# Tile 1 of a sparse expert layer moves from a fully dense to a half-gathered, half-dense form

## The chip, the cores and the metric

The kernel runs on one core of a Trainium2 chip. The metric is the device time of one execution in microseconds. Five engines work beside each other: TensorE (PE: matmuls, with PEld its weight loads), VectorE (DVE), ScalarE (ACT), GpSimd (POOL) and SyncE (SP, which here only issues DMAs). Each engine runs its own instructions strictly in the order in which the built program holds them.

## The reference, cut to what matters

One encoder layer over 1024 tokens of 1024 features: an attention and pooling block, then the PEER layer that the change is about. Each token picks 128 of 16384 experts (8 heads, 16 each), each with a gate.

```
q = (ht @ wq).reshape(T, PEER_HEADS, 2, PEER_HALF)
sc = jnp.einsum('thpd,hpnd->thpn', q, subkeys, preferred_element_type=jnp.float32)
...
u = jnp.take(u_tab, eb, axis=0)
vv = jnp.take(v_tab, eb, axis=0)
act = jax.nn.gelu(jnp.einsum('tkd,td->tk', u, xb), approximate=False)
return jnp.einsum('tk,tkd->td', gb * act, vv)
```

The first product is u times token, the second is the sum of the v rows weighted by gate times activation.

## The kernel before

The tokens are eight tiles of 128. Each tile's PEER layer is done in one of two ways.

- **Gathered** (tiles 0, 6, 7): for each of the 128 picks, GpSimd issues an indirect DMA that brings one u row (4 KB) for each of the 128 tokens into a row buffer (512 KB a gather, line 165), and VectorE multiplies it with the token's vector and sums (line 186). Then 128 gathers of v rows, which VectorE adds into the output with a weight (line 193). That is 256 gathers a tile. The row buffers form a ring, and a gather into a buffer waits until VectorE has done with the buffer's last row. The ring has two buffers in the first part (GB0), three (GBUFS: two named row, one rowx) once `wide` is set, and six in the last part. The gathers of all tiles stand in one list, in order, and `flow(x)` takes the next of them at a given rate between other work.
- **Dense** (tiles 1 to 5): all 16384 experts are computed, in 128 blocks of 128. `u_mm(b)` multiplies a block of u with the five tiles' 640 tokens, as two halves of 320 columns, each 24 matmuls (three terms of a split fp32 product, eight chunks of the features). The Gelu of it is multiplied with the gates, which `gates(i)` has written as a dense table (expert, token) to DRAM as `gd`, and `v_chunk` multiplies the results of four blocks with v: for each of the five tiles and each half of the features 12 matmuls of 512 columns (line 966). ACT splits u into a rounded part, and GpSimd makes the rest (line 240).

The program runs through these stages: **front** (first product `first`, attention and output projection `second` for groups of tiles; tile 0's routing `zero` beside the tiles 1 and 2), **scores** (the routing products of the other seven tiles, with `top16` on VectorE), **gates** (for each tile in ORDER: `topk`, and for a dense tile `gates`), **back** (the dense blocks with `u_mm`, `v_chunk`). 68 of the 128 u blocks are computed ahead of the back (`ahead()`), beside scores and gates, and kept in DRAM as `ad`. A list scheduler with a timeline of its own fixes each engine's order when the program is built, so the order of one engine can be read, and differs from the order of the source.

The lines that the steps rest on:

```
issue(n + GBUFS - 1 + (XBUFS if st.get("more") else 0))
r = rows.pop(n)
vec = st["vec"]
if s == 0:
    V.scalar_tensor_tensor(r, r, 1.0, vec, op0=OP.mult, op1=OP.mult, accum_out=st["act"][:, k:k + 1])
```

Of the kernel before, what the change touches and what calls it, by code (L numbers as in the profile page):

```python
# [31 lines left out]
GSCALE = 32768.0  # L32
EARLY = 0.2
EARLY2 = 0.4
EARLY3 = 0.45
ORDER = (6, 1, 2, 3, 4, 5, 7)
PER = 8
# [3 lines left out]
YS = 26  # L41
# [7 lines left out]
ULP = 4  # L49
FIRST = ((0, 1, 2), (3, 4), (5, 6), (7,))  # L50
ZN = 80
# [4 lines left out]
SPLIT0 = 1  # L56
AT = (-1, 0, 2, 3)
GB0 = 2
# [9 lines left out]
XT = 1  # L68
LOS = (1, 1, 2, 2)
LOS2 = (1, 1, 1, 2, 1)  # L70
# [14 lines left out]
GATHERED = (0, 6, 7)  # L85
DENSE = (1, 2, 3, 4, 5)
ND = len(DENSE)
DT = ND * P
NH = DT // 2
GBUFS = 3  # L90
# [33 lines left out]
def body(tc, ctx, a):  # L124
# [20 lines left out]

    gathers = [(i, s, k) for i in GATHERED for s in range(2) for k in range(128)]
    tabs = (a["u"], a["v"])
# [22 lines left out]
    def gather_step():  # L170
# [14 lines left out]
        if s == 0:  # L185
            V.scalar_tensor_tensor(r, r, 1.0, vec, op0=OP.mult, op1=OP.mult, accum_out=st["act"][:, k:k + 1])  # L186
            if k == P - 1:
                gl = st["G"].tile([P, P], F32, name="act", bufs=2)
                S.activation(gl, st["act"], AF.Gelu)
                V.tensor_tensor(gl, gl, EX[i][1], op=OP.mult)  # L190
                st["gl"] = gl
# [25 lines left out]
    after = dict(zip([None] + soon + later, soon + later + [None]))  # L217
    ad = DR.tile([KEYS, P, DT], F32, name="ad")

# [33 lines left out]
    def open_u():  # L253
        B = U["u"] = ctx.enter_context(tc.tile_pool(name="dense", bufs=1, side="right", reuse_waits="tile"))
        hh = U["hh"] = B.tile([P, DC, DT], F32R, name="hh")
        hl = U["hl"] = B.tile([P, DC, DT], F32R, name="hl")
        for j, i in enumerate(DENSE):
            halves(i, hh[:, :, j * P:(j + 1) * P], hl[:, :, j * P:(j + 1) * P])
        return hh, hl

    def u_mm(b):
        uh, ul = (t.rearrange("p (c e) -> p c e", c=DC) for t in us.pop((b, None)))
        pa = []
        after["turn"] = not after.get("turn")
        for n in range(2):
            p = PS.tile([P, 512], F32, name="pu", bufs=2) if b in soon or after["turn"] else ps()
            for k, (l, r) in enumerate(((uh, U["hh"]), (uh, U["hl"]), (ul, U["hh"]))):
                for d in range(DC):
                    E.matmul(p[:, :NH], l[:, d, :], r[:, d, n * NH:(n + 1) * NH],  # L269
                             start=(k == 0 and d == 0), stop=(k == 2 and d == DC - 1))  # L270
            pa.append(p)
        return pa

    def ahead():
        if AHEAD:
            with tc.high_priority(offset=-AHP):
                load(after[None])
                split(after[None])
        for b in soon:
            with tc.high_priority(offset=-AHP):  # L280
                if after[b] is not None:
                    load(after[b])
                pa = u_mm(b)
                if after[b] is not None:
                    split(after[b])
                t = U["u"].tile([P, DT], F32, name="wr", bufs=WRB)
                for n in range(2):
                    S.activation(t[:, n * NH:(n + 1) * NH], pa[n][:, :NH], AF.Gelu)  # L288
                nc.scalar.dma_start(ad[b], t)
            yield  # L290
# [10 lines left out]
def front(tc, ctx, a, env):  # L301
# [84 lines left out]
    def late_consts():  # L386
# [218 lines left out]
    def second(tiles):  # L605
# [22 lines left out]
        for m, i in enumerate(tiles):  # L628
# [28 lines left out]
    def topk(i):  # L657
# [29 lines left out]
        for s in range(2):  # L687
# [13 lines left out]
            yield  # L701
        keep = i in GATHERED
        gate = (C if keep else X).tile([P, PH, 16], F32, name=f"gate{i}" if keep else "gate", bufs=1)
# [11 lines left out]
        if keep:  # L715
            EX[i] = (idx, gate.rearrange("p h r -> p (h r)"))
        else:
            p = ps()
# [11 lines left out]
    def scores(tiles, cols, split):  # L730
# [45 lines left out]
        for i in tiles:  # L776
            carry["top", i] = vv[i], ix[i]

    def gates(i):
        j = DENSE.index(i)  # L780
        ekT, gT = carry["G", i]
        for q in range(P // TCH):
            sg = M.tile([P, KEYS, TCH], F32, name="stage", bufs=2)
            for r in range(TCH // 8):
                t0 = q * TCH + r * 8

                pairs = lambda x: x.rearrange("p (q w) -> p q w", w=2)[:, :, None, :].to_broadcast([P, 4, P, 2])
                ob = []
                for s in range(2):
                    o = M.tile([P, 4, P, 2], F16, name=f"ob{s}", bufs=OB)  # L790
                    V.tensor_tensor(o, pairs(ekT[:, s, t0:t0 + 8]), late["iote"][:, None, :, :].to_broadcast([P, 4, P, 2]),  # L791
                                    op=OP.is_equal)
                    ob.append(o)
                yield
                og = []
                for s in range(2):
                    o = M.tile([P, 4, P, 2], F16, name=f"og{s}", bufs=OB)
                    V.tensor_tensor(o, ob[1], pairs(gT[:, s, t0:t0 + 8]), op=OP.mult)  # L798
                    og.append(o)
                yield  # L800
                for h in range(2):
                    p = ps()
                    for t in range(4):
                        for s in range(2):
                            E.matmul(p[:, t * KEYS:(t + 1) * KEYS], ob[0][:, h * 2 + t // 2, :, t % 2], og[s][:, h * 2 + t // 2, :, t % 2],
                                     start=(s == 0), stop=(s == 1))
                    S.activation(sg[:, :, r * 8 + h * 4:r * 8 + h * 4 + 4], p.rearrange("p (t e) -> p e t", t=4),
                                 AF.Copy, scale=1.0 / GSCALE)
                yield
# [55 lines left out]
    X.open("late")  # L865
    rest = GATHERED[1:]
# [4 lines left out]
    cols = [(hh[:, :, :NH], hl[:, :, :NH]), (hh[:, :, NH:], hl[:, :, NH:]), (gh, gl)]  # L871
    merge([(scores(DENSE + rest, cols, True), 2 * PH * (NT - 1 + 3)), (ahead, AHEAD1)], EARLY2)
# [15 lines left out]
def back(tc, ctx, a, env):  # L888
# [34 lines left out]
    def u_block(b):  # L923
        if b not in soon and after[b] is not None:
            load(after[b])
        if b % CHUNK == 0 and b // CHUNK + 1 < NCH:
            gload(b // CHUNK + 1)
        wr = B.tile([P, DT], F32, name="wb", bufs=WB)
        if b in soon:
            nc.sync.dma_start(wr, ad[b])  # L930
            pa = [wr]
        else:
            pa = [p[:, :NH] for p in u_mm(b)]
            pace(2)
            if after[b] is not None:
                split(after[b])
            for n in range(2):
                S.activation(pa[n], pa[n], AF.Gelu)
            pace(1)
        g = gts[b // CHUNK]  # L940
        wh = B.tile([P, DT], F32R, name="wh", bufs=CHUNK + WX)
        wl = B.tile([P, DT], F32R, name="wl", bufs=CHUNK + WX)
        w, hn = DT // len(pa), NTC // len(pa)
        for n, p in enumerate(pa):
            V.tensor_tensor(wr[:, n * w:(n + 1) * w].rearrange("p (n t) -> p n t", t=TCH),  # L945
                            p.rearrange("p (n t) -> p n t", t=TCH),
                            g[:, n * hn:(n + 1) * hn, b % CHUNK, :], op=OP.mult)
        m = b % CHUNK
# [3 lines left out]
        S.activation(wh, wr, AF.Copy)  # L952
        pace(3 if b not in soon else 0.5)
        V.tensor_tensor(wl, wr, wh, op=OP.subtract)  # L954
# [84 lines left out]
```

## Time and profile before

| | us |
|---|---|
| median of 3 runs | 2683.09 (2680.38 to 2690.16) |
| the profiled execution's own time | 2683.19 |
| its span, first to last instruction | 2681.3 |
| busy in the span: PE, DVE, POOL, ACT | 2483.0, 2295.3, 1412.3, 925.3 |

The span is what the stages below are cut from; 1.9 us lie around it. A busy share of an engine is an average over stages: what ends last in a stage is read from that stage. Matmuls are pipelined, so the time of one is longer than the step from one to the next.

### The profile page before, as it was taken

What the parts mean: (1) busy time and instruction counts of PE and PEld (TensorE: products, weight loads), DVE (VectorE), ACT (ScalarE), POOL (GpSimd) and SP (SyncE); (2) the same over time, 40 slices, a digit from 0 to 9 for tenths busy, and PEclk for the clock granted to TensorE, in tenths of its full rate; (3) what the DMA queues carried; (4) which work ended last, traced back from release to release, by engine and by line L of the source; (5) the groups of instructions that cost most, each with busy time, mean ns of one, the idle gap of its engine ahead of it and who ended that gap; (6) DMA issues with size and microseconds to landing.
All of it is one profiled execution on the core that took longest, in us unless ns stands there. A gap on an engine that the chain in (4) does not pass through costs nothing.

```text
span 2681.3 us, 41366 instructions
## 1 busy us (share of the span) xinstructions
PE 2483.0 (93%) x14627; PEld 2198.3 (82%) x14627; DVE 2295.3 (86%) x4668; ACT 925.3 (35%) x1699; POOL 1412.3 (53%) x1380
## 2 busy tenths in 40 slices
PE   7889886999989789888959999999999999999999
PEld 6657654999988789887858888888888888888887
DVE  4657776679989899997959999899998998989998
ACT  5744553432223344444423222222223222222221
POOL 1101566665556665656645565465564655645653
PEclk9889988999999899999979999999999999999999
DMA  7645578987778776878799999899998999989987
GB/s 246 208 146 182 190 255 261 336 297 233 242 230 262 239 224 209 261 243 260 240 356 342 358 348 328 322 339 333 346 350 316 359 357 331 346 313 359 345 315 264
DMA packets 321504, 770.23 MB, mean 287 GB/s; under 512 B 26736, under 2 KB 123920, under 8 KB 317200
## 3 DMA queue, kind: packets, MB, share of 16 engines
q0 software_dynamic: 110592, 402.70, 42.3%
q1 hardware_dynamic: 114352, 287.55, 31.0%
q10 hardware_dynamic: 96352, 77.34, 8.9%
q8 instruction: 114, 1.87, 0.3%
q14 instruction: 94, 0.77, 0.1%
HBM read 687.53 MB, written 79.95 MB: 286 GB/s over the span
## 4 chain that ended last, share of the span: by engine, by line
PE 60%; DVE 18%; DMA 10%; issue 3%; POOL 2%; ACT 1%; ACTq 1%; SPq 0%; DVEq 0%; POOLq 0%
PE pt L966 15%; PE ps L966 15%; PE pu L269 14%; PE pt L269 3%; PE ps L269 3%; DMA row<-u,idx 3%; DVE vec L193 3%; DVE og L798 3%; DVE ob L791 2%; PE pt L360 2%; DVE row L186 2%; DMA row<-v,idx 1%; DMA wb<-ad 1%; DMA rowx<-v,idx 1%; DMA ad<-wr 1%
## 5 line engine op out<-in xcount | busy, mean ns | idle before, releaser
L240 POOL TENSOR_TENSOR ul<-ur,uh 128x256 fp32r<-128x256 f32 x512 | 456.7, 923 | 155.4 <-ACT uh L235 74.0
L165 POOL DMA_INDIRECT row<-v,idx x301 | 329.2, 1094 | 337.7 <-DVE vec L193 218.3
L165 POOL DMA_INDIRECT row<-u,idx x306 | 315.1, 1030 | 295.7 <-DVE row L186 169.2
L193 DVE SCALAR_TENSOR_TENSOR vec<-row,act,vec 128x1024 f32<-128x1024 f32 x301 | 384.9, 1279 | 36.0 <-DMA row<-v,idx 33.8
L186 DVE SCALAR_TENSOR_TENSOR row<-row,vec 128x1024 f32<-128x1024 f32 x306 | 368.0, 1211 | 37.6 <-DMA row<-u,idx 37.6
L269 PE MATMUL pu<-hh,uh 128*128 128x320 f32 x1568 | 282.7, 319 | 39.9 <-ACT wr L288 39.8
L269 PEld LDWEIGHTS pu<-hh,uh 128*128 128x128 f32 x1568 | 246.7, 193 | 53.4 <-ACT wr L288 47.5
L269 PE MATMUL pu<-hh,ul 128*128 128x320 f32 x1568 | 278.7, 314 | 5.8 <-POOL ul L240 5.8
L269 PE MATMUL pu<-hl,uh 128*128 128x320 f32 x1568 | 283.0, 317 | 0.0
L269 PEld LDWEIGHTS pu<-hh,ul 128*128 128x128 f32 x1568 | 243.9, 191 | 11.9 <-POOL ul L240 7.4
L269 PEld LDWEIGHTS pu<-hl,uh 128*128 128x128 f32 x1568 | 248.2, 193 | 2.6
L235 ACT ACTIVATE uh<-ur 128x1024 fp32r<-128x1024 f32 x128 | 135.5, 1059 | 266.6 <-PE pu L269 193.6
L966 PE MATMUL pt<-v0h,wh 128*128 128x512 f32 x384 | 151.9, 396 | 30.8 <-ACT wh L952 26.1
L952 ACT ACTIVATE wh<-wb 128x640 fp32r<-128x640 f32 x128 | 92.0, 733 | 246.0 <-DVE wb L945 126.3
L235 ACT ACTIVATE v0h<-vr 128x512 fp32r<-128x512 f32 x128 | 80.5, 631 | 246.9 <-DMA vr<-v 135.1
L966 PE MATMUL pt<-v0h,wl 128*128 128x512 f32 x384 | 151.8, 395 | 3.2 <-DVE wl L954 3.0
L966 PE MATMUL pt<-v0l,wh 128*128 128x512 f32 x384 | 150.4, 392 | 0.0
L966 PE MATMUL ps<-v1h,wh 128*128 128x512 f32 x384 | 149.5, 389 | 0.0
L966 PE MATMUL ps<-v1h,wl 128*128 128x512 f32 x384 | 149.5, 389 | 0.0
L966 PE MATMUL ps<-v1l,wh 128*128 128x512 f32 x384 | 149.5, 389 | 0.0
L165 POOL DMA_INDIRECT rowx<-v,idx x83 | 89.6, 1080 | 98.6 <-DVE vec L193 45.9
L969 DVE TENSOR_TENSOR acc<-pt,acc 128x512 f32<-128x512 f32 x160 | 109.3, 683 | 36.7 <-PE pt L966 36.4
(265 smaller groups left out, 5867.5 us busy)
## 6 DMA issues: line engine op xcount, KB each, us to landing
ur<-uT SPq DMA_DIRECT2D x128, 512.0 KB, 5.0
vr<-v SPq DMA_DIRECT2D x256, 256.0 KB, 5.9
gd<-stage ACTq DMA_DIRECT2D x20, 2048.0 KB, 12.3
g<-gd SPq DMA_DIRECT2D x32, 1280.0 KB, 9.2
ad<-wr ACTq DMA_DIRECT2D x68, 320.0 KB, 4.9
wb<-ad SPq DMA_DIRECT2D x68, 320.0 KB, 6.7
wo<-w_out SPq DMA_DIRECT2D x80, 256.0 KB, 4.0
wi<-w_in SPq DMA_DIRECT2D x32, 512.0 KB, 4.8
```

The lines of the kernel that those rows point to most:

```text
L165: Q.indirect_dma_start(out=r, out_offset=None, in_=tabs[s], in_offset=bass.IndirectOffsetOnAxis(ap=EX[i][0][:, k:k + 1], axis=0))
L186: V.scalar_tensor_tensor(r, r, 1.0, vec, op0=OP.mult, op1=OP.mult, accum_out=st["act"][:, k:k + 1])
L193: V.scalar_tensor_tensor(vec, r, st["gl"][:, k:k + 1], vec, op0=OP.mult, op1=OP.add)
L235: S.activation(hi, t, AF.Copy)
L240: Q.tensor_tensor(lo[:, part], t[:, part], hi[:, part], op=OP.subtract)
L269: E.matmul(p[:, :NH], l[:, d, :], r[:, d, n * NH:(n + 1) * NH], start=(k == 0 and d == 0), stop=(k == 2 and d == DC - 1))
L360: E.matmul(p, x[l][:, d, :], w[r][:, dd], start=(d == 0 and k == 0), stop=(d == DC - 1 and k == len(terms) - 1))
L791: V.tensor_tensor(o, pairs(ekT[:, s, t0:t0 + 8]), late["iote"][:, None, :, :].to_broadcast([P, 4, P, 2]), op=OP.is_equal)
L798: V.tensor_tensor(o, ob[1], pairs(gT[:, s, t0:t0 + 8]), op=OP.mult)
L952: S.activation(wh, wr, AF.Copy)
L966: E.matmul(p, l[:, j * P:(j + 1) * P], r, start=(m == 0 and k == 0), stop=(m == CHUNK - 1 and k == 2))
L969: V.tensor_tensor(acc[:, j, hf * 512:(hf + 1) * 512], p, acc[:, j, hf * 512:(hf + 1) * 512], op=OP.add)
```

## The change

Tile 1 is still dense in the second product, but its first product is gathered, like that of the tiles 0, 6 and 7. Its 128 u gathers stand in the list behind tile 0's 256. When they are done, `mixed_parts` splits gate times activation into three bf16 parts, and `gates(MIXED)` writes that product to `gd` in place of the gates, in three matmul terms where the other tiles take two. `u_mm` then has four tiles: 512 columns in one half. Tile 1 stands first in ORDER, and `gates(MIXED)` is emitted with the last tile of ORDER, 7, since the gathers have to be done by then; the loop in it takes gather after gather until they are. In the front, tile 0 now runs alone first (FIRST, AT), its attention and routing are one chain beside `first` of the tiles 1 and 2, and the gathers' rates are other numbers.

```
-EARLY = 0.2
-EARLY2 = 0.4
-EARLY3 = 0.45
-ORDER = (6, 1, 2, 3, 4, 5, 7)
+EARLY = 0.7
+EARLY2 = 0.5
+EARLY3 = 0.5
+ORDER = (1, 2, 3, 6, 4, 5, 7)
...
-FIRST = ((0, 1, 2), (3, 4), (5, 6), (7,))
+FIRST = ((0,), (1, 2), (3, 4), (5, 6), (7,))
...
-DENSE = (1, 2, 3, 4, 5)
+MIXED = 1
+BYU = (2, 3, 4, 5)
+DENSE = (MIXED,) + BYU
...
-    gathers = [(i, s, k) for i in GATHERED for s in range(2) for k in range(128)]
+    gathers = [(i, s, k) for i, n in ((0, 2), (MIXED, 1), (6, 2), (7, 2)) for s in range(n) for k in range(128)]
...
-        for n in range(2):
-            p = PS.tile([P, 512], F32, name="pu", bufs=2) if b in soon or after["turn"] else ps()
-            for k, (l, r) in enumerate(((uh, U["hh"]), (uh, U["hl"]), (ul, U["hh"]))):
-                for d in range(DC):
-                    E.matmul(p[:, :NH], l[:, d, :], r[:, d, n * NH:(n + 1) * NH],
-                             start=(k == 0 and d == 0), stop=(k == 2 and d == DC - 1))
+        p = PS.tile([P, 512], F32, name="pu", bufs=2)
+        for k, (l, r) in enumerate(((uh, U["hh"]), (uh, U["hl"]), (ul, U["hh"]))):
+            for d in range(DC):
+                E.matmul(p, l[:, d, :], r[:, d, :], start=(k == 0 and d == 0), stop=(k == 2 and d == DC - 1))
...
+    def mixed_parts():
+        ekT, _ = carry["G", MIXED]
+        p = ps()
+        E.transpose(p[:, :P], env["st"]["glm"], ident)
+        gT = X.tile([P, 3, P], BF16, name="gM", bufs=1)
+        S.activation(gT[:, 0, :], p[:, :P], AF.Copy)
+        left = X.tile([P, P], F32, name="tm", bufs=1)
+        V.tensor_tensor(left, p[:, :P], gT[:, 0, :], op=OP.subtract)
+        S.activation(gT[:, 1, :], left, AF.Copy)
+        V.tensor_tensor(gT[:, 2, :], left, gT[:, 1, :], op=OP.subtract)
+        carry["G", MIXED] = (ekT, gT)
...
     def gates(i):
         j = DENSE.index(i)
+        if i == MIXED:
+            while "glm" not in env["st"]:
+                env["gather_step"]()
+                yield
+            mixed_parts()
+            yield
...
-    merge([A2(GROUPS[1]), (lift(zero(), HPZ), ZN)] + firsts(1), 0)
+    merge([(chain(second(GROUPS[0]), lift(zero(), HPZ)), YS + ZN)] + firsts(0), 0)
     X.close()
     open_g()
+    merge([A2(GROUPS[1])] + firsts(1), EARLY)
...
-        if i in DENSE:
+        if i in BYU:
             parts = [(chain(topk(i), gates(i)), 12 + 4 * 13)]
+        elif i == ORDER[-1]:
+            parts = [(chain(topk(i), gates(MIXED)), 12 + 4 * 13)]
...
-    rate = (len(gathers) - st["done"]) / (KEYS * 12.0 - AHEAD * 5.5)
+    rate = (len(gathers) - st["done"]) / (KEYS * 10.8 - AHEAD * 4.3)
```

Where instructions stand. On VectorE, at the end of the gates stage, the order before is this (L698 and L699 belong to tile 7's `topk`, L707 writes its expert numbers, L193 is a v gather's sum, L242 the split of a v block, L945 the first product with the gates in the back):

```order
L699 TENSOR_TENSOR e_14583<-hit_14613 128x64
L193 SCALAR_TENSOR_TENSOR vec<-row,act,vec 128x1024
L707 SCALAR_TENSOR_TENSOR idx_14622<-e_14583 128x128
L193 SCALAR_TENSOR_TENSOR vec<-row,act,vec 128x1024
L193 SCALAR_TENSOR_TENSOR vec<-rowx,act,vec 128x1024
L193 SCALAR_TENSOR_TENSOR vec<-row,act,vec 128x1024
L242 TENSOR_TENSOR v0l<-vr,v0h 128x512 x3
L945 TENSOR_TENSOR wb<-wb,g 128x640
```

At the same place of the changed kernel (L697 and L705 are those two rows of tile 7, L195 is the sum of tile 0's v gathers) it is this:

```order
L697 TENSOR_TENSOR e_12352<-hit 128x64
L195 SCALAR_TENSOR_TENSOR vec<-row,act,vec 128x1024
L705 SCALAR_TENSOR_TENSOR idx_12394<-e_12352 128x128
L195 SCALAR_TENSOR_TENSOR vec<-row,act,vec 128x1024
L195 SCALAR_TENSOR_TENSOR vec<-rowx,act,vec 128x1024
L195 SCALAR_TENSOR_TENSOR vec<-row,act,vec 128x1024 x2
```

Behind L705 stand 158 gather rows with nothing between them: 30 of tile 0's v gathers, then all 128 u gathers of tile 1 (L188). They end so (glm is gate times activation of tile 1, gM its three parts, og the gate table's factor for eight tokens, ob the one-hot factor):

```order
L188 SCALAR_TENSOR_TENSOR rowx,act<-rowx,vec 128x1024
L188 SCALAR_TENSOR_TENSOR row,act<-row,vec 128x1024 x2
L192 TENSOR_TENSOR glm<-glm,gate_9459 128x128
L792 TENSOR_TENSOR tm<-pt,gM 128x128
L824 TENSOR_TENSOR og_12551<-ob_12546,gM 128x1024
L188 SCALAR_TENSOR_TENSOR rowx,act<-rowx,vec 128x1024
L794 TENSOR_TENSOR gM<-tm,gM 128x128
```

From glm to the first product of the back (L973) VectorE has 48 rows og, 22 rows ob and 15 gathers. So before, a few gathers stood here, and 244 of 768 were done when the back began; now 401 of 896 are.

On TensorE the last gates of a tile and the rows behind them were these before (L805 is the gate table's matmul, L269 `u_mm` of blocks of the back):

```order
L805 MATMUL ps<-og_14481,ob_14477 128x128
L805 LDWEIGHTS ob_14477
L805 MATMUL ps<-og_14483,ob_14477 128x128
L269 MATMUL pu<-hh,ul 128x320 x4
L269 MATMUL pu<-hh,uh 128x320 x7
```

Now they are these (L831 is the gate table's matmul, L788 the transposition of glm):

```order
L831 LDWEIGHTS ob_12243
L831 MATMUL ps<-og_12252,ob_12243 128x128
L788 MATMUL pt<-ident,glm 128x128
L831 LDWEIGHTS ob_12544
L831 MATMUL ps<-og_12551,ob_12544 128x128
```

Behind the last matmul of tile 5's table comes the transposition of glm at once, and tile 1's 384 matmuls behind it. 70 of the 128 u blocks stand ahead of it, the same number as stood ahead of the back's first v product before. On GpSimd the gathers number 226 to 401 stand without a row of line 240 (of the changed kernel: 242) between them.

At the program's start TensorE had three tiles' matmuls for each pair of weights before (pu, pu and vec are the tiles 0, 1, 2):

```order
L360 MATMUL pu<-wih,xh 128x512
L360 MATMUL pu<-wih,xl 128x512
L360 MATMUL vec<-wih,xh 128x512
L360 MATMUL vec<-wih,xl 128x512
L360 MATMUL pu<-wil,xh 128x512 x2
L360 MATMUL vec<-wil,xh 128x512
```

Now it has tile 0's alone, and the tiles 1 and 2 come with a second pass over the same weights:

```order
L356 MATMUL pu<-wih,xh 128x512
L356 MATMUL pu<-wih,xl 128x512
L356 MATMUL pu<-wil,xh 128x512
L413 MATMUL ps<-w_142,prob 128x384
L413 MATMUL pt<-w_142,prob 128x384
```

## Rows read from the trace of the kernel before

**Rows 1.** The page: span, and busy time of each engine.

```profile
span 2681.3 us, 41366 instructions
PE 2483.0 (93%) x14627; PEld 2198.3 (82%) x14627; DVE 2295.3 (86%) x4668; ACT 925.3 (35%) x1699; POOL 1412.3 (53%) x1380
```

**Rows 2.** Busy time by window: start, scores, gates, turn, back; TensorE's clock, DMA.

```profile
core 0: us, PE busy (x) PEld busy (x) DVE busy (x) ACT busy (x) POOL busy (x), PEclk, DMA share, GB/s
0.00:20.00 20.00, 7.92 (x26) 5.94 (x27) 9.18 (x34) 12.20 (x33) 1.30 (x6) 1.00 0.89 296
20.00:40.00 20.00, 19.47 (x85) 13.63 (x84) 8.68 (x23) 11.42 (x23) 0.88 (x1) 1.00 1.00 354
0.00:540.00 540.00, 455.35 (x2337) 354.10 (x2338) 350.85 (x822) 269.93 (x628) 199.24 (x183) 0.92 0.69 228
540.00:811.00 271.00, 255.44 (x1837) 251.16 (x1836) 241.04 (x1047) 72.31 (x130) 152.19 (x147) 1.00 0.76 252
811.00:1340.00 529.00, 468.69 (x3743) 448.68 (x3743) 493.12 (x1114) 226.40 (x370) 324.70 (x289) 0.96 0.75 241
1340.00:1372.00 32.00, 13.70 (x92) 13.17 (x90) 11.72 (x15) 6.77 (x10) 17.14 (x21) 0.75 1.05 390
1372.00:2681.00 1309.00, 1289.78 (x6624) 1131.17 (x6624) 1198.61 (x1671) 349.84 (x562) 719.02 (x742) 1.00 0.92 335
```

**Rows 3.** The chain that ended last, in order of time: start, us, what.

```profile
1423.51 3.52 PE ps L269 x24
...
2582.93 2.75 PE pt L966 x12
```

**Rows 4.** The page's costliest groups: VectorE's sums over gathered rows (count, busy, mean ns, idle).

```profile
L193 DVE SCALAR_TENSOR_TENSOR vec<-row,act,vec 128x1024 f32<-128x1024 f32 x301 | 384.9, 1279 | 36.0 <-DMA row<-v,idx 33.8
L186 DVE SCALAR_TENSOR_TENSOR row<-row,vec 128x1024 f32<-128x1024 f32 x306 | 368.0, 1211 | 37.6 <-DMA row<-u,idx 37.6
```

**Rows 5.** VectorE's waits from 811 to 1340 us: total, times, longest.

```profile
DVE vec L193 <- DMA row<-v,idx: 11.1, 8, 2.9
DVE vec L193 <- DMA rowx<-v,idx: 9.5, 5, 5.1
DVE gate L704 <- PE pt L721: 5.1, 1, 5.1
DVE ob L791 <- PE pt L805: 4.7, 1, 4.7
```

**Rows 6.** Timeline of GpSimd, then of VectorE, 534 to 543 us.

```profile
535.50 0.96 POOL L165 DMA_INDIRECT rowx<-u,idx  x1 [1.44 <-DVE rowx L186]
...
534.00 1.22 DVE L186 SCALAR_TENSOR_TENSOR rowx<-rowx,vec 128x1024 f32<-128x1024 f32 x1 [2.65 <-DMA rowx<-u,idx]
535.15 0.08 DVE L186 DVE_READ_ACCUMULATOR rowx<-rowx,vec 128x1 f32 x1
535.23 1.22 DVE L186 SCALAR_TENSOR_TENSOR row<-row,vec 128x1024 f32<-128x1024 f32 x1
536.38 0.08 DVE L186 DVE_READ_ACCUMULATOR row<-row,vec 128x1 f32 x1
537.20 1.22 DVE L186 SCALAR_TENSOR_TENSOR row<-row,vec 128x1024 f32<-128x1024 f32 x1 [0.75 <-DMA row<-u,idx]
538.35 0.08 DVE L186 DVE_READ_ACCUMULATOR row<-row,vec 128x1 f32 x1
541.79 1.22 DVE L186 SCALAR_TENSOR_TENSOR rowx<-rowx,vec 128x1024 f32<-128x1024 f32 x1 [3.36 <-DMA rowx<-u,idx]
```

**Rows 7.** The row buffer's gathers from 545 to 725 us: issue to landing.

```profile
DMA to landing us min/median/max: 4.2/5.2/8.8
```

**Rows 8.** The same, from 1020 to 1180 us.

```profile
DMA to landing us min/median/max: 5.1/7.3/9.3
```

**Rows 9.** DMA queues of the page: packets, MB, time as a share of 16 engines.

```profile
q0 software_dynamic: 110592, 402.70, 42.3%
```

**Rows 10.** Timeline of VectorE in the gates stage: start, us of the merged row.

```profile
1097.77 8.82 DVE L791 TENSOR_TENSOR ob<-ekT,iote 128x1024 f16<-128x1024 f16 x8
...
1106.84 1.27 DVE L193 SCALAR_TENSOR_TENSOR vec<-row,act,vec 128x1024 f32<-128x1024 f32 x1
1108.03 0.26 DVE L650 MAX8 best<-cand 128x8 f32<-128x112 f32 x1
1108.22 1.26 DVE L798 TENSOR_TENSOR og<-ob,gT 128x1024 f16<-128x1024 f16 x2
1109.41 0.26 DVE L650 MAX8 best<-cand 128x8 f32<-128x112 f32 x1
```

**Rows 11.** Groups by line and form, 728 to 1340 us: the gates' og and ob.

```profile
L798 DVE TENSOR_TENSOR og<-ob,gT 128x1024 f16<-128x1024 f16 x160 | 119.2, 801 | 0.0
L791 DVE TENSOR_TENSOR ob<-ekT,iote 128x1024 f16<-128x1024 f16 x160 | 116.7, 769 | 4.7 <-PE pt L805 4.7
```

More of the change, by code (lines that the diff above doesn't have):

```diff
@@ L56 @@
 SPLIT0 = 1
-AT = (-1, 0, 2, 3)
+AT = (-1, 0, 1, 2, 3)
 GB0 = 2
@@ L187, in gather_step @@
             if k == P - 1:
-                gl = st["G"].tile([P, P], F32, name="act", bufs=2)
+                gl = C.tile([P, P], F32, name="glm", bufs=1) if i == MIXED else st["G"].tile([P, P], F32, name="act", bufs=2)
                 S.activation(gl, st["act"], AF.Gelu)
                 V.tensor_tensor(gl, gl, EX[i][1], op=OP.mult)
-                st["gl"] = gl
+                st["glm" if i == MIXED else "gl"] = gl
         else:
@@ L282, in ahead @@
                     load(after[b])
-                pa = u_mm(b)
+                p = u_mm(b)
                 if after[b] is not None:
                     split(after[b])
-                t = U["u"].tile([P, DT], F32, name="wr", bufs=WRB)
-                for n in range(2):
-                    S.activation(t[:, n * NH:(n + 1) * NH], pa[n][:, :NH], AF.Gelu)
+                t = U["u"].tile([P, NU], F32, name="wr", bufs=WRB)
+                S.activation(t, p, AF.Gelu)
                 nc.scalar.dma_start(ad[b], t)
@@ L716, in topk @@
             EX[i] = (idx, gate.rearrange("p h r -> p (h r)"))
+            if i == MIXED:
+                p = ps()
+                for s in range(2):
+                    E.transpose(p[:, s * P:(s + 1) * P], e12[:, s, :], ident)
+                ekT = X.tile([P, 2, P], BF16, name="ekM", bufs=1)
+                S.activation(ekT.rearrange("p s t -> p (s t)"), p[:, :2 * P], AF.Copy)
+                carry["G", i] = (ekT, None)
         else:
@@ L795, in gates @@
                 og = []
-                for s in range(2):
-                    o = M.tile([P, 4, P, 2], F16, name=f"og{s}", bufs=OB)
+                for s in range(np_):
+                    o = M.tile([P, 4, P, 2], dt, name=f"og{s % 2}", bufs=OB)
                     V.tensor_tensor(o, ob[1], pairs(gT[:, s, t0:t0 + 8]), op=OP.mult)
@@ L870, in front @@
         env["halves"](i, gh[:, :, m * P:(m + 1) * P], gl[:, :, m * P:(m + 1) * P])
[L871 to L872 removed]
+    cols = [(hh, hl), (gh, gl)]
+    merge([(scores(BYU + rest, cols, True), 2 * PH * (NT - 1 + 2)), (ahead, AHEAD1)], EARLY2)
     M.close()
@@ L928, in u_block @@
         wr = B.tile([P, DT], F32, name="wb", bufs=WB)
+        g = gts[b // CHUNK]
+        nm = DT - NU
+        S.activation(wr[:, :nm].rearrange("p (n t) -> p n t", t=TCH), g[:, :nm // TCH, b % CHUNK, :], AF.Copy)
         if b in soon:
-            nc.sync.dma_start(wr, ad[b])
-            pa = [wr]
-        else:
-            pa = [p[:, :NH] for p in u_mm(b)]
-            pace(2)
+            p = wr[:, nm:]
+            nc.sync.dma_start(p, ad[b])
+        else:
+            p = u_mm(b)
+            pace(1.6)
             if after[b] is not None:
                 split(after[b])
[L937 to L940, printed above, removed]
+            S.activation(p, p, AF.Gelu)
+            pace(0.8)
         wh = B.tile([P, DT], F32R, name="wh", bufs=CHUNK + WX)
         wl = B.tile([P, DT], F32R, name="wl", bufs=CHUNK + WX)
[L943 to L947, printed above, removed]
+        V.tensor_tensor(wr[:, nm:].rearrange("p (n t) -> p n t", t=TCH), p.rearrange("p (n t) -> p n t", t=TCH),
+                        g[:, nm // TCH:, b % CHUNK, :], op=OP.mult)
         m = b % CHUNK
@@ L952, in u_block @@
         S.activation(wh, wr, AF.Copy)
-        pace(3 if b not in soon else 0.5)
+        pace(2.4 if b not in soon else 0.5)
         V.tensor_tensor(wl, wr, wh, op=OP.subtract)
```

44 lines of the change are left out of this document (23 added, 21 removed).

## The prediction

> **What bounds the kernel now.** I read the page first for the busy shares: TensorE 93%, VectorE 86% of 2681.3 us [rows 1]. No engine has much to give, and the change loads VectorE with 128 more gathers and frees TensorE, so shares alone say little. Cut into stages [rows 2], the picture is this. In the front (0 to 540) TensorE is busy 455 of 540 us. From 540 to 811 (scores) it is busy 255 of 271 and VectorE 241. From 811 to 1340 (gates) VectorE is busy 493 of 529 and TensorE 469: VectorE is the tighter one, and of its 36 idle us 20.6 went to waits for gathered rows and 9.8 to waits for TensorE [rows 5]. From 1340 to 1372 nearly all stand still: the last gate table has to go out to DRAM and come back before the back can start. In the back TensorE is busy 1290 of 1309 us and VectorE 1199: TensorE sets its length.
>
> **The back: TensorE's saving.** In the chain, 24 matmuls of 320 columns take 3.52 us, and a block of u needs 48, so 7.04 us; 12 matmuls of 512 columns take 2.75 us [rows 3], so the 24 that a block needs now take 5.50. That is 1.54 us a block. 58 blocks stand in the back before and after (70 of 128 stand ahead of it in both orders): 58 x 1.54 = 89 us. By the order VectorE has 495 gathers left there instead of 524, 29 x 1.2 = 35 us, and its product with the gates is a fifth narrower, an estimate of 20 us over 128 blocks; so it falls to some 1144 of its 1199 us, in 1220: 94% where it was 92%. Some of the saving will be lost to that tightness. I take **-79**, with -89 as the best and -43 as the worst (VectorE at 90% would need 1144 / 0.90 = 1271).
>
> **The front: tile 0 alone.** In the first 40 us the DMA engines are full (0.89 and 1.00) while TensorE does 27.4 us of work for three tiles [rows 2]. With one tile the same weights have to come in, and a third of that work is done; 18 us of it go to later, with a second pass over the weights, into a stage where TensorE is busy 84% of the time: 18 / 0.84 = 21. I take **+20**. Tile 0's routing will be done earlier, but the order shows that little is made of it: when the last tile's normed tokens are ready, 70 gathers stand before it on VectorE, against 60. Bounds: -10 (the earlier gathers close idle time) to +45 (the chain of tile 0 stands alone for as long again).
>
> **Scores.** Between that row and the first `topk`, VectorE now has 75 gathers instead of 94: 19 fewer, at a step of 1.2 us (534.00 to 535.23 [rows 6]) 23 us; the eight u blocks ahead give TensorE 8 x 1.54 = 12. With both engines near their limit I take **-18**.
>
> **Gates, up to tile 7's expert numbers.** VectorE loses 22 rows ob, 32 rows og (one tile's gates are now later) and 9 gathers. At 0.77 and 0.80 us a row [rows 11], less the 0.08 that a row's end overlaps the next (1106.84 + 1.27 to 1108.03 [rows 10]), that is 15 + 23 + 11 = 49 us of 493. TensorE loses more (a tile's table, and 1.54 us a block), so it does not take over. The idle time by waits for TensorE may shrink. I take **-53**; -110 if the stage followed TensorE instead, -40 if VectorE's waits for rows grow.
>
> **The 158 gathers that now stand alone.** This is the term that decides. By the order, VectorE runs 158 gather rows with nothing between them, behind tile 7's expert numbers, because the gates of tile 1 need all 128 of its u gathers, and they stand behind tile 0's in the list. On TensorE nothing is left: the last table of tile 5 is done by then, and what follows is the transposition of glm, which waits for the last of the 158. GpSimd has no work of line 240 between them. So this stretch is covered by nothing, and its length is added whole. Before, such gathers stood between VectorE's other rows, and the time from issue to landing was hidden there.
>
> What does one cost? The ring has three buffers in this stage, so three gathers go round together. A round is: VectorE's row (1.21 us, line 186, or 1.28, line 193 [rows 4], the first with 0.08 for reading the sum), then the issue on GpSimd 0.27 us later (535.23 to 535.50 [rows 6]), then issue to landing. Rows 6 hold one such round as it is: the rowx buffer is read at 534.00, two other buffers follow, and rowx is read again at 541.79, after VectorE had waited 3.36 us. 7.79 us for three gathers is 2.60 each. But the DMA engines were then also bringing in u blocks and weights. From issue to landing the median is 5.2 us and the least 4.2 in the scores stage [rows 7], at a DMA share of 0.76; in the gates stage it is 7.3 [rows 8], with u blocks in and tables out. In the new stretch gathers are nearly alone. I take 4.7, between the least and the median of rows 7: (4.7 + 0.27 + 1.29) / 3 = 2.09 us, and 158 x 2.09 = 330. The change of tile in the middle (the vector of tile 0 copied out, that of tile 1 in) costs some 5. **+335.** Bounds: 158 x (4.2 + 1.56) / 3 = 303 and 158 x 2.60 = 411. It cannot be below what the transfers themselves take: 768 gathers used 42.3% of the 16 engines' span [rows 9], 1134 us, so 1.48 us each, 234 in all.
>
> The Trainium skill has a price for this, in "DMA: Bandwidth & Descriptors", section "Anatomy of one DMA — SWDGE (gpsimd) path": a DMA issued by GpSimd takes about 2.0 us and its bytes at 436 GB/s, which for 512 KB is an estimate of 3.2 us. By it a round would be 3.2 + 1.56 = 4.8 us, the stretch 251 us, and the sum below 79 us less. In rows 7 no gather landed in less than 4.2 us, so the trace does not agree, and the sum goes by the rows [rows 7].
>
> **Tile 1's table, behind it.** VectorE has 22 ob, 48 og and 15 gathers. Where GpSimd runs no subtraction beside them, two og take 1.19 us (1108.22 to 1109.41) and a gather 1.19 (1106.84 to 1108.03); eight ob in a row took 8.82 elsewhere [rows 10]. With GpSimd idle I take 0.61: 70 x 0.61 + 15 x 1.19 = 61. Gelu, transposition and the three parts go one after another across ACT, TensorE and VectorE, some 5 us. **+66**, and 80 at the means of rows 11. TensorE has 384 matmuls there where another tile has 256, and waits for VectorE; that its clock falls while it idles (it was granted 0.75 in the turn [rows 2]) then costs nothing. The turn to the back stands as before, with one more table as its last: **+2**.
>
> **Sum.** +20 - 18 - 53 + 335 + 66 + 2 - 79 = +273, against the profiled execution's own 2683 us (span 2681.3 and 1.9 around it; the median of the runs, 2683.09, is the same): **2956, say 2955 us**, 10% slower.
>
> **Rivals.**
> - *The lone gathers go at the transfers' pace.* With nothing else on the DMA engines the landing shrinks until the 1.48 us of transfer rule: 234 + 5 instead of 335, so 2859. For it speaks that the quietest landings (4.2) were still measured beside other traffic; against it, that three buffers would need a round of 4.4 us, and so a landing of 2.9, which no row shows. Chance 0.14. The Trainium skill's price above, with its sum of 2877, lies near this rival.
> - *The lone gathers land as in the gates stage.* 7.3 us: (7.3 + 1.56) / 3 = 2.95, 466 us, so 3091. Against it speaks that the u blocks and tables which made the landings long there are done. Chance 0.12.
> - *Not slower: the lone gathers are covered.* If tile 1's gathers overlapped the u blocks ahead, as those of tile 0 did before, the 335 would go away and 2621 remain, the saving that fewer columns give. The point from which it decides is 335 - 273 = 62 us for the stretch, 0.39 us a gather. Against it stands the order: an engine cannot take a later row first, and VectorE alone needs 1.2 us a row. Chance 0.04, for an order that I misread.
> - *The front or the gates stage gives back much more.* TensorE's freed time pulls the gates stage to -110 and the front to -10: 2868. VectorE's 93% there speaks against it. Chance 0.08.
>
> **How the numbers follow.** The forecast, with landings of 4.2 to 5.7 us and each other term near its value, has 0.62 and spans 2900 to 3015. The range goes on to the fast rivals below and part of the slow one above: **2855 to 3030**. A measurement of this kernel can tell about 0.5% from no change. Faster by over 0.5% has 0.03 and within 0.5% 0.01, both from the covered case; slower has 0.96.
>
> **What would show it.** Right: in the profile after, VectorE has about 158 rows of the gather lines in one stretch of 300 to 365 us, somewhere from 1290 to 1625 us, mostly waiting for DMA of row and rowx, with TensorE idle in it; then a table of some 65 us; then a back of 1220 to 1250 us with TensorE busy 97% or more. The chain of what ended last runs through DMA row<-u and VectorE there. u_mm steps at 229 ns a matmul. Wrong: a stretch much shorter than 300 us, TensorE with u blocks beside it, a back that VectorE sets (TensorE under 95%), or a front that is over 45 us longer.

## The result: 3046.01 us, 13% slower

The changed kernel takes 3046.01 us (median, 3035.22 to 3046.66), the kernel before 2686.19 us beside it: the ratio is 1.133, 95% interval [1.130, 1.137]. The prediction had the sign and the main cause, but its 2955 us is 91 us short, and its range ended 16 us below the result.

The page of the changed kernel, its span, busy times and, of the 40 slices, TensorE and its clock (it answers to [rows 1]):

```profile
span 3044.9 us, 35302 instructions
...
PE 2330.2 (77%) x11299; PEld 1876.6 (62%) x11299; DVE 2497.3 (82%) x4904; ACT 941.0 (31%) x1706; POOL 1518.2 (50%) x1508
...
PE   5698967899878988810000359999999999999999
...
PEclk9799988899999998855555779999999999999999
```

TensorE lost 153 us of work, VectorE gained 202, and there is a hole in TensorE's slices. By window (start, scores, gates, the hole, tile 1's table, the turn, the back; columns as in [rows 2]):

```profile
0.00:576.00 576.00, 451.86 (x2134) 340.54 (x2135) 378.62 (x856) 276.46 (x635) 201.48 (x187) 0.89 0.69 228
576.00:836.50 260.50, 235.02 (x1200) 202.77 (x1200) 224.96 (x1026) 68.98 (x106) 132.04 (x120) 0.97 0.69 227
836.50:1329.00 492.50, 398.44 (x2351) 319.00 (x2349) 470.79 (x1065) 203.67 (x294) 324.02 (x310) 0.90 0.76 243
1329.00:1688.00 359.00, 0.00 (x0) 0.00 (x0) 195.82 (x286) 2.32 (x3) 147.14 (x158) 0.50 0.74 235
1688.00:1752.00 64.00, 30.19 (x385) 27.76 (x385) 60.17 (x103) 20.10 (x36) 19.88 (x18) 0.83 0.74 238
1752.00:1779.00 27.00, 0.00 (x0) 0.00 (x0) 5.69 (x9) 3.44 (x7) 3.96 (x4) 0.55 0.95 342
1779.00:3044.90 1265.90, 1214.68 (x5232) 986.49 (x5232) 1161.23 (x1564) 366.05 (x627) 689.73 (x713) 0.99 0.90 328
```

In the fourth row TensorE does nothing for 359 us (it had stopped 20 us earlier), GpSimd issues 158 gathers, and VectorE is busy little over half. The page's groups name the wait (idle before, and what ended it; the first line counts the whole kernel):

```profile
L188 DVE SCALAR_TENSOR_TENSOR row<-row,vec 128x1024 f32<-128x1024 f32 x424 | 511.0, 1214 | 179.3 <-DMA row<-u,idx 170.7
...
L788 PE MATMUL pt<-ident,glm 128*128 128x128 f32 x1 | 0.5, 475 | 379.3 <-DVE glm L192 379.3
```

One round of the ring in that stretch, in the timeline of GpSimd and VectorE (it answers to [rows 6]), and the landing times of tile 1's gathers into the row buffer, 1400 to 1680 us (to [rows 7, 8]):

```profile
1420.62 1.22 DVE L188 SCALAR_TENSOR_TENSOR rowx<-rowx,vec 128x1024 f32<-128x1024 f32 x1 [1.28 <-DMA rowx<-u,idx]
1421.77 0.08 DVE L188 DVE_READ_ACCUMULATOR rowx<-rowx,vec 128x1 f32 x1
1422.12 0.94 POOL L167 DMA_INDIRECT rowx<-u,idx  x1 [1.57 <-DVE rowx L188]
...
1426.98 1.22 DVE L188 SCALAR_TENSOR_TENSOR rowx<-rowx,vec 128x1024 f32<-128x1024 f32 x1 [0.73 <-DMA rowx<-u,idx]
```

```profile
DMA to landing us min/median/max: 4.0/5.1/5.7
```

The buffer is read at 1420.62, issued again at 1422.12 and read again at 1426.98: 6.36 us for three gathers. All engines wait for the round trip: VectorE for the row, GpSimd for VectorE to free a buffer.

The scores stage ends, in both kernels, with the first `topk`. The same row of it, before and now:

```profile
811.56 0.67 DVE L661 TENSOR_TENSOR cand<-vv 128x512 f32<-128x512 f32 x1
```

```profile
836.46 0.67 DVE L659 TENSOR_TENSOR cand<-vv 128x512 f32<-128x512 f32 x1
```

By landmarks (last normed tokens at 530.1 and 575.9 us, this `cand` row, the end of the gates stage, glm, the last table's way out, first product with v), the difference of the two spans, some 363 us, divides into front +46, scores -21, gates -36, lone gathers +359.5, tile 1's table +64, turn -7.5 and back -41.6. The gates stage ends with its last table's way out before (1339.6) and with tile 7's expert numbers now (1328.6). Taken to those numbers before too (1346.4), gates is -43 and the turn -1. By the other `cand` row of that `topk` (802.2 and 831.2 us) scores is -17, and the gates are 4 us the better.

### The profile page after: what moved, and what is told of

It is laid out like the page before. It is cut to its first block, busy times and chain, and to the rows that moved or that the text cites. A ratio compares the mean times of both kernels' runs of the same rounds, so it can differ in the third digit from the quotient of the medians.

```text
span 3044.9 us, 35302 instructions
## 1 busy us (share of the span) xinstructions
PE 2330.2 (77%) x11299; PEld 1876.6 (62%) x11299; DVE 2497.3 (82%) x4904; ACT 941.0 (31%) x1706; POOL 1518.2 (50%) x1508
## 5 line engine op out<-in xcount | busy, mean ns | idle before, releaser
L188 DVE SCALAR_TENSOR_TENSOR row<-row,vec 128x1024 f32<-128x1024 f32 x424 | 511.0, 1214 | 179.3 <-DMA row<-u,idx 170.7
L242 POOL TENSOR_TENSOR ul<-ur,uh 128x256 fp32r<-128x256 f32 x512 | 447.6, 907 | 100.4 <-issue 40.2
L195 DVE SCALAR_TENSOR_TENSOR vec<-row,act,vec 128x1024 f32<-128x1024 f32 x299 | 382.6, 1280 | 33.1 <-DMA row<-v,idx 31.0
L268 PE MATMUL pu<-hh,uh 128*128 128x512 f32 x1024 | 277.2, 413 | 45.1 <-ACT wr L284 37.5
L788 PE MATMUL pt<-ident,glm 128*128 128x128 f32 x1 | 0.5, 475 | 379.3 <-DVE glm L192 379.3
L268 PE MATMUL pu<-hh,ul 128*128 128x512 f32 x1024 | 265.3, 393 | 6.1 <-POOL ul L242 6.1
L268 PE MATMUL pu<-hl,uh 128*128 128x512 f32 x1024 | 265.3, 397 | 0.0
L788 PEld LDWEIGHTS pt<-ident,glm 128*128 128x128 f32 x1 | 0.2, 182 | 379.6 <-DVE glm L192 379.6
L993 PE MATMUL ps<-v0h,wh 128*128 128x512 f32 x384 | 155.6, 405 | 50.1 <-ACT wh L979 45.9
L993 PE MATMUL ps<-v0h,wl 128*128 128x512 f32 x384 | 154.9, 403 | 13.4 <-DVE wl L981 13.2
L979 ACT ACTIVATE wh<-wb 128x640 fp32r<-128x640 f32 x128 | 91.7, 732 | 203.4 <-PE pt L993 142.1
L993 PE MATMUL ps<-v0l,wh 128*128 128x512 f32 x384 | 152.3, 397 | 0.0
L993 PE MATMUL pt<-v1h,wh 128*128 128x512 f32 x384 | 149.4, 389 | 0.0
L993 PE MATMUL pt<-v1h,wl 128*128 128x512 f32 x384 | 149.4, 389 | 0.0
L993 PE MATMUL pt<-v1l,wh 128*128 128x512 f32 x384 | 149.4, 389 | 0.0
```

The source lines that it names most:

```text
L242: Q.tensor_tensor(lo[:, part], t[:, part], hi[:, part], op=OP.subtract)
L268: E.matmul(p, l[:, d, :], r[:, d, :], start=(k == 0 and d == 0), stop=(k == 2 and d == DC - 1))
L788: E.transpose(p[:, :P], env["st"]["glm"], ident)
L993: E.matmul(p, l[:, j * P:(j + 1) * P], r, start=(m == 0 and k == 0), stop=(m == CHUNK - 1 and k == 2))
```

## Experiments

In every run that is told as an edit, the rest is the changed kernel; differences of stages are against its trace.

**1. A larger ring.**

```diff
-GBUFS = 3
-XBUFS = 3
+GBUFS = 5
+XBUFS = 1
```

> Edit: five gather buffers instead of three from the gates and scores stage on; in the back the ring has six as before the edit. By the order 98 gathers then stand alone behind tile 7's expert numbers instead of 158, since 60 more come before them. Theory (the ring sets the pace of the lone gathers, landing plus 1.56 us for three buffers): with five buffers the pace falls from 2.28 us to that of the transfers, 1.65 to 1.8 us, so the stretch takes about 172 us instead of 359.5; the 60 gathers moved ahead cost 40 to 72 us on VectorE; the time is 2900 to 2930 us. Rival (something that more buffers do not help, an issue or transfer rate of about 2.2 us a gather, sets the pace): the pace stays at 2.2 to 2.3, the stretch is about 220 us for the 98, and the time is 2945 to 2975 us. The pace in the stretch decides.

Measured: 2899.75 us, ratio to before 1.080 [1.075, 1.086], at the fast end of the theory's range. The stretch:

```profile
1413.50:1564.50 151.00, 0.00 (x0) 0.00 (x0) 120.69 (x198) 0.30 (x1) 91.08 (x98) 0.50 0.95 345
```

98 gathers in 151.0 us are 1.54 us each, where three buffers gave 359.5 / 158 = 2.28. The DMA share rises from 0.74 to 0.95, so the DMA engines are now nearly full, and the pace is better than the 1.65 to 1.8 expected. The rival, a fixed rate of 2.2, falls. The stretch gives back 208.5 us; the 60 gathers that moved ahead of it show as tile 7's numbers 85 us later (24 of them a longer front). The back, from its first product with v, is 23 us shorter (1243 instead of 1266), with VectorE busy 1133 us in it instead of 1161.

**2. Four buffers**, to try the same law between three and five.

```diff
-GBUFS = 3
-XBUFS = 3
+GBUFS = 4
+XBUFS = 2
```

> Edit: four gather buffers from the scores stage on (the back has six as before the edit). By the order 131 gathers stand alone instead of 158. Theory (pace = landing plus 1.56 us, over the number of buffers, until the transfers' own 1.5 us is reached): landings of 5.1 to 5.6 us give (5.1 + 1.56) / 4 = 1.67 to 1.79 us a gather, a stretch of 219 to 235 us, and 2930 to 2970 us in all. Rival (three buffers were enough for most of it and the fifth did the work): 2.0 us or more a gather, over 262 us.

Measured: 2977.38 us, ratio 1.111 [1.106, 1.116].

```profile
1361.50:1603.80 242.30, 0.00 (x0) 0.00 (x0) 161.20 (x261) 2.36 (x3) 121.85 (x131) 0.50 0.85 289
```

242.3 / 131 = 1.85 us a gather: above the theory's 1.67 to 1.79, well under the rival's 2.0, and the time is a little over what was expected. Solved for the landing, pace x buffers - 1.56 gives 5.3, 5.8 and 6.1 us for three, four and five buffers: by this law a gather lands later the more are on the way. Only for three buffers does a trace show landings (median 5.1); the other two figures are worked out, not measured.

**3. Tile 1's gathers earlier in the list.**

```diff
-gathers = [... for i, n in ((0, 2), (MIXED, 1), (6, 2), (7, 2)) for s in range(n) ...]
+gathers = [... for i, s in ((0, 0), (MIXED, 0), (0, 1), (6, 0), (6, 1), (7, 0), (7, 1)) ...]
```

> Edit: tile 1's first-product gathers stand in the list ahead of tile 0's second-product gathers. By the order 48 gathers then stand alone instead of 158, and the back has 614 instead of 483, of which 109 come behind the last row of the dense work. Theory (the stretch is as long as the gathers that stand in front of tile 1's weights; moved into the back they cost VectorE's time, which is the tighter engine there): the stretch takes 48 x 2.275 = 109 us, 250 less; the back takes 125 to 160 us more; the time is 2900 to 2950 us. Rival (VectorE does not set the back, the moved gathers hide under TensorE): the back stays below 1300 us and the time is about 2800 us.

Measured: 2932.51 us, ratio 1.092 [1.088, 1.097]. The lone stretch is 110.2 us for 48 gathers (2.30 each, theory 109), 249 less; the back, from its first sum into acc to the end, is 1389.5 us instead of 1235.7, 154 more. Both as the theory had them: a gather taken out of the stretch costs VectorE elsewhere. The added time stands bare at the end, where TensorE has nothing left:

```profile
2781.00:2934.00 153.00, 0.56 (x3) 0.13 (x1) 141.36 (x111) 1.02 (x1) 97.55 (x104) 0.51 0.96 374
```

**4. The front put back.**

```diff
-FIRST = ((0,), (1, 2), (3, 4), (5, 6), (7,))
-AT = (-1, 0, 1, 2, 3)
-LOS = (1, 1, 1, 2, 2)
+FIRST = ((0, 1, 2), (3, 4), (5, 6), (7,))
+AT = (-1, 0, 2, 3)
+LOS = (1, 1, 2, 2)
...
+    merge([A2(GROUPS[0])] + firsts(0), 0)
...
-    merge([(chain(second(GROUPS[0]), lift(zero(), HPZ)), YS + ZN)] + firsts(0), 0)
+    merge([A2(GROUPS[1]), (lift(zero(), HPZ), ZN)] + firsts(1), 0)
...
-    merge([A2(GROUPS[1])] + firsts(1), EARLY)
```

> Edit: only the front is put back (three tiles first, tile 0 routed beside the other tiles' second half); the mixed tile stays. Theory (tile 0 alone costs the front 46 us and little of it comes back): the last tile's normed tokens are ready near 530 us instead of 576, four more gathers stand alone (+9 us), and 54 gathers instead of 70 stand ahead of that row, which cost at most 16 x 1.2 = 19 us later: 3010 to 3030 us. Rival (the 46 us are given back later whatever the front does, since the number of gathers done by then sets the stretch): 3040 us or more.

Measured: 3003.24 us, ratio 1.119 [1.113, 1.125], 43 less than the changed kernel and under the expected 3010. The last normed tokens come at 539.9 us, 36 earlier; the rival, that it is given back, falls. The first 180 us, of the changed kernel:

```profile
0.00:180.00 180.00, 118.17 (x576) 91.30 (x577) 93.69 (x269) 89.11 (x217) 12.35 (x16) 0.87 0.68 225
```

and with the old front:

```profile
0.00:180.00 180.00, 148.18 (x691) 110.60 (x692) 101.52 (x256) 103.47 (x258) 24.77 (x21) 0.89 0.62 205
```

With tile 0 alone TensorE has done 30 us less by then.

**5. No gathers for tile 1.** The table is made from the plain gates, so tile 1's activations are left out.

```diff
-    gathers = [... for i, n in ((0, 2), (MIXED, 1), (6, 2), (7, 2)) for s in range(n) ...]
+    gathers = [... for i in GATHERED for s in range(2) ...]
...
-        E.transpose(p[:, :P], env["st"]["glm"], ident)
+        E.transpose(p[:, :P], EX[MIXED][1], ident)
...
-            while "glm" not in env["st"]:
-                env["gather_step"]()
-                yield
```

> Edit: tile 1's first product is left out: no gathers for it and no wait, its table is made from the plain gates in three bf16 parts, so that its rows of the output lack the activations. Theory (the lone gathers are the whole loss; the other terms of the sum, as measured, cancel to about +4 us): the time is 2660 to 2720 us, no better than before the change. Rival (the saving of columns would show if nothing waited, as the prediction's sum without the gathers has it): about 2620 us or less.

Measured: 2764.38 us, ratio 1.030 [1.026, 1.033]. Neither the theory nor the rival: 44 us over the theory's range. The lone stretch is gone, but tile 1's table now lies in the gates stage (tile 7's numbers 56 us later) and the back, from its first sum into acc, takes 1316 us instead of 1236, with 38 more gathers in it. Two rows of that back:

```profile
1444.00:2716.00 1272.00, 1206.04 (x5141) 975.60 (x5139) 1150.14 (x1566) 356.63 (x612) 687.63 (x714) 0.98 0.91 324
2716.00:2760.00 44.00, 0.00 (x0) 0.00 (x0) 36.70 (x29) 1.02 (x1) 21.39 (x23) 0.56 0.84 322
```

In the last 44 us the remaining gathers run with TensorE done. So even a free first product would not have made the kernel faster in this form; the theory's sum lacked VectorE in the back, which the next three runs look at.

**6. Tile 7 without its second product.** Its v gathers, sums and output rows are left out.

```diff
-... ((0, 2), (MIXED, 1), (6, 2), (7, 2)) ...
+... ((0, 2), (MIXED, 1), (6, 2), (7, 1)) ...
```

> Edit: tile 7's second product is left out (its 128 v gathers, their sums and its output rows), so that the back has 355 gathers instead of 483. Theory (in the back VectorE, busy 1161 of 1266 us, keeps TensorE waiting): with 155 us of VectorE's work gone TensorE sets the back, 1215 busy us at 98.5%, 1233 us, so the time is 3005 to 3020 us. Rival (the missing 37 us of the back come from elsewhere, the order of the product's four-block steps or ACT's halves): the back stays near 1266 and the time is 3040 us or more.

**7. The same sums, slim.**

```diff
+            w = slice(0, 64 if i == 7 else D)
-            V.scalar_tensor_tensor(vec, r, st["gl"][:, k:k + 1], vec, op0=OP.mult, op1=OP.add)
+            V.scalar_tensor_tensor(vec[:, w], r[:, w], st["gl"][:, k:k + 1], vec[:, w], op0=OP.mult, op1=OP.add)
```

> Edit: tile 7's 128 second-product sums on VectorE work on 64 of the 1024 columns, so that its output rows lack the rest; all gathers, issues and transfers stay. It parts VectorE from the DMA engines, which in the back are busy 0.9 of the time. Theory (VectorE's time): some 128 x 1.1 = 140 us of VectorE's work are gone and the time falls as in the run without these gathers, 3005 to 3025 us. Rival (transfers and their issue on GpSimd keep the rows late, and with them the row queue of VectorE): the time stays within 10 us of 3045.

Measured: 3036.00 us (ratio 1.130 [1.126, 1.135]) and 3031.67 us (1.129 [1.124, 1.133]), some 10 and 14 less than the change, the first no more than runs of one kernel differ by: by the time alone the theory missed. The windows say why. These rows stand only in the last 350 us of the back. Of 300 us there, of the change and then of the slim run:

```profile
2679.00:2979.00 300.00, 293.78 (x1272) 238.67 (x1272) 285.22 (x330) 89.30 (x153) 172.73 (x174) 0.99 0.93 338
```

```profile
2678.00:2978.00 300.00, 298.44 (x1303) 245.18 (x1304) 186.03 (x339) 89.91 (x158) 168.47 (x175) 0.99 0.92 339
```

TensorE's idle time falls from 6.2 to 1.6 us with the DMA share unchanged, but there were only 6 us to win in this place.

**8. All gather sums of the back, slim** (64 of 1024 columns, for tiles 6 and 7 in both products).

```diff
+        w = slice(0, 64 if st.get("more") else D)
...
-            V.scalar_tensor_tensor(r, r, 1.0, vec, ..., accum_out=st["act"][:, k:k + 1])
+            V.scalar_tensor_tensor(r[:, w], r[:, w], 1.0, vec[:, w], ..., accum_out=st["act"][:, k:k + 1])
-            V.scalar_tensor_tensor(vec, r, st["gl"][:, k:k + 1], vec, ...)
+            V.scalar_tensor_tensor(vec[:, w], r[:, w], st["gl"][:, k:k + 1], vec[:, w], ...)
```

> Edit: every gather's sum that VectorE does in the back works on 64 of the 1024 columns (tiles 6 and 7 lack the rest in both products); all gathers, issues and transfers stay. In the run that slimmed tile 7's second product alone those rows stood in the last 350 us of the back only, and TensorE's idle time there fell from some 2.5 to under 1 us in 100. Theory (VectorE's gather rows in the back cost TensorE its 4 us in 100, and the clock that it loses by it): with VectorE at 0.55 to 0.65 all along, TensorE is idle 1 us in 100 or less, the back takes 1220 to 1235 us instead of 1266, and the time is 3005 to 3020 us. Rival (the shorter u product is to blame, since TensorE reaches the product with v before the halves wh and wl are there, whatever else VectorE does): TensorE still idles 3 to 5 us in 100 in the first 900 us of the back, and the time stays at 3025 to 3045.

Measured: 3006.70 us, ratio 1.120 [1.116, 1.123], in the theory's range. From its first product with v the back takes 1223.1 us instead of 1265.9, at a DMA share of 0.92. Two windows of the change, and the same two of this run:

```profile
1879.00:1979.00 100.00, 93.16 (x400) 75.41 (x399) 91.44 (x141) 26.69 (x45) 53.21 (x57) 0.98 0.94 342
...
2379.00:2479.00 100.00, 93.06 (x397) 74.91 (x396) 91.26 (x147) 27.60 (x48) 52.18 (x55) 0.98 0.92 332
```

```profile
1879.00:1979.00 100.00, 99.98 (x442) 82.41 (x441) 52.47 (x149) 30.66 (x52) 58.71 (x62) 1.00 0.94 346
...
2379.00:2479.00 100.00, 99.98 (x441) 82.48 (x440) 57.88 (x145) 32.26 (x54) 55.68 (x59) 1.00 0.94 350
```

TensorE's waits in the back of the change say through what:

```profile
PE ps L993 <- ACT wh L979: 45.9, 12, 27.4
PE ps L993 <- DVE wl L981: 13.2, 15, 2.4
PE pu L268 <- DVE wb L973: 7.5, 8, 1.3
```

27.4 of the first row is the turn; the rest and the rows below it are the parts of the gated product, of which VectorE makes wb and wl, and ScalarE makes wh out of wb. So VectorE's work made TensorE idle; the rival, that the shorter u product is to blame, falls. All transfers are still there, at a share as high as before, so it was not the DMA engines either.

**9. The three edits that helped, together** (five buffers, the list of run 3, the old front).

> Edit: the three edits together: five gather buffers from the scores stage on, tile 1's first-product gathers ahead of tile 0's second-product ones, and the front of before. By the order tile 1's weights are then ready two rows behind tile 7's expert numbers, 11 gathers stand alone, and the back has 608 gathers, 107 of them behind its last row. Theory (VectorE carries the added gathers wherever they stand): the stretch's 359.5 us go to about 25, the front gives 42, the gates stage takes 35 to 50 more for 30 more gathers, the back 125 to 155 more: 2825 to 2880 us, still slower than before the change. Rival (the wait was the whole cost, and gathers in the back hide under TensorE): 2690 to 2720 us.

Measured: 2863.48 us, ratio 1.066 [1.062, 1.071], in the theory's range. Tile 1's weights are ready 6.4 us behind tile 7's numbers, so the lone stretch is gone, and the back takes 1390.8 us (1235.7 with the change, from its first sum into acc), of which the last 149 have VectorE alone, with 107 gathers. VectorE is busy 2500 us in all, as in the change (2497): nothing was saved there, only moved.

**10. The kernel before with four buffers**, as a control.

```diff
-GBUFS = 3
-XBUFS = 3
+GBUFS = 4
+XBUFS = 2
```

> Edit to the kernel before the change: four gather buffers instead of three from the scores stage on (five do not fit beside its wider pool of the dense tiles); in the back six as before. Theory (before the change other rows stand between the gathers, so the ring is hidden there): of the 45 us that VectorE waits for rows in scores and gates some part closes, and the time is 2650 to 2685 us. Rival (the ring paces the gathers there too): 2640 us or less. In neither case is the 8% between the change and the change with five buffers seen here.

Measured: 2673.01 us (2661.72 to 2689.35) beside 2684.93 for three, ratio 0.996 [0.994, 0.999]: 0.4% less, at the edge of what this kernel's measurement tells from no change, and in the theory's range. Where other rows stand between the gathers, the ring is nearly hidden; with the change, where they stand alone, the fourth buffer saved 69 us (3046 to 2977). No version with the change that computes the whole result came below 2863.

## Why the prediction was right in sign and short in size

- **The lone gathers: forecast +335, measured +359.5.** Right in kind: 158 of them, one stretch, ring of three, TensorE idle throughout, which runs 1 to 3 confirm from three sides. The step that was off is the landing: "I take 4.7, between the least and the median". It was 5.1, and the round (5.1 + 0.27 + 1.29) / 3 = 2.22 gives 351; the change of tile and some longer rounds make the rest. The quiet that was expected to shorten the landing did not: three gathers at once keep the DMA engines 0.74 busy by themselves. The estimate of 251 us by the price of the Trainium skill ("DMA: Bandwidth & Descriptors", "Anatomy of one DMA — SWDGE (gpsimd) path") lies farther off; the 3.2 us estimated from it for one gather was reached by none of the 158 (least 4.0).
- **The back: forecast -79, measured -41.6,** the largest miss. The step that failed: "TensorE sets its length", with a margin of 10 us for VectorE at 94%. Of the 89 us that fewer columns were to save, 48 were lost: TensorE stood idle 51 us there instead of 18, and its work fell by 75 us, not 89. VectorE does 1161 us of work in the back (1144 were forecast), and the back takes 1266: 91.7%, the share that it had before (1198.6 of 1309, [rows 2]). Run 8 takes most of VectorE's gather work out (some 690 us busy instead of 1161) and returns 42.8 us, so that the back is 84 shorter than before the change, near the forecast's best case of 89. A part of the loss is TensorE's clock: granted 1.00 in nearly all of the back before, 0.97 or 0.98 in five of twelve windows of 100 us of the change, in each of which TensorE was idle 2 to 7 us; the products with v took 911.0 us instead of 901.0 for the same 3840 matmuls, and 897.5 in run 8. The stated worst case of -43 was nearest, and in part by luck: its own 1271 us (VectorE at 90%) is 38 below 1309, not 43, and VectorE had more work at a higher share. Why VectorE's share stays there is not shown. Up to TensorE's end it was 0.90 to 0.93 in the back of the kernel before and of runs 1 to 5 and 9, yet single windows of the change go higher with TensorE nearly full:

```profile
2179.00:2279.00 100.00, 98.81 (x432) 80.20 (x430) 97.78 (x111) 30.38 (x51) 61.44 (x61) 1.00 0.96 348
```

- **The front: forecast +20, measured +46** (43 in time, run 4). The step that failed: "18 us of it go to later", read off the first 40 us. TensorE is behind by 30 us at 180 (118.2 against 148.2 busy). By the order, tile 0's second half and its routing have few other tiles beside them for that long; no run parts this from the rest of the old front. The bound of +45 was named and missed by one.
- **Gates: forecast -53, measured -36** (-43 to tile 7's numbers), about at the bound of -40. The step that failed is VectorE's saving, "15 + 23 + 11 = 49 us of 493". It lost 22 (492.1 to 470.4 us busy). The 32 rows og and 22 rows ob went as counted, but 3 gathers fewer stand there instead of 9 (6 to tile 7's numbers), and the rows that are left take longer: 856 ns instead of 801 for og, 803 instead of 769 for ob. Why they do is not shown; GpSimd is busy 0.66 of the stage, where it was 0.61. VectorE's idle time fell from 36 to 22 us.
- **Scores -21 (forecast -18), tile 1's table +64 (+66)** were close. In the scores VectorE's busy time fell from 246.6 to 225.1 us, as the 19 gathers fewer had it, though its waits for u rows rose from 16 to 28. In the table rows og and ob followed each other every 0.60 us, as taken (0.61). The **turn** came out at -7.5 (+2).

The four misses (26 + 17 + 24.5 + 37) all lie on the slow side, 105 us, the other three give 14 back, and the sum is 91 over. The gathers lay inside their stated bounds, the back and the front within 2 us of theirs, the gates 4 us beyond theirs; the range took most terms at their middle and only one at its end. Of the signs that the prediction named, the stretch of 300 to 365 us and the table came. The back missed its 1220 to 1250 us at 97% (TensorE is at 96.0%), and the front's +46 is past the 45 that was named as a sign of being wrong.

The rival "not slower" needed the gathers covered. Runs 5 and 9 show that this would not have been enough in any arrangement tried: the 128 gathers are 155 us of VectorE's time, in a kernel where VectorE is already busy 0.96 of the gates stage and 0.92 of the back.

## What to carry to other kernels

A wait that stands alone is priced by its round trip over the number of buffers; look for the ring's size first, and for what VectorE must do anyway if the wait is cured. An engine that is busy 92% beside the one that sets the pace is not spare: trading its time for the other's moves the bound. Here the share at which it stood before was a better guess of its share after than a denser packing. When several terms share one bias (here, an engine called free), the range must take them at their bad ends together.

## What the runs showed of the hardware that was not expected

- Indirect gathers of 128 rows of 4 KB that stand alone paced at 2.28, 1.85 and 1.54 us with three, four and five buffers, at DMA shares of 0.74, 0.85 and 0.95 (235, 289 and 345 GB/s). That share is not one fixed pace: at the ends of runs 3 and 9, with six buffers, gathers came every 1.40 and 1.39 us at 0.96 (374 and 376 GB/s), where VectorE's row alone takes 1.28. The Trainium skill ("DMA: Bandwidth & Descriptors", "Anatomy of one DMA — SWDGE (gpsimd) path") puts the data term at 436 GB/s, an estimate of 1.20 us a gather; the traces do not reach it, and no stretch of gathers alone here came under 1.39 (107 in 149 us at the end of run 9).
- TensorE's clock was granted 0.50, the 1.2 GHz level, all through the lone stretch, and still 0.83 on average in the 64 us behind it, while the table's matmuls waited for VectorE anyway.
